# Layer 1's experts: weights in 8 KB pieces with tokens in that order, and tokens of seven of eight pairs fetched by indirect loads

## The chip, the cores and the metric

The kernel runs on one core of one Trainium2 chip, in float32. The metric is the device time of one execution in microseconds (us), lower is better, given as the median of the runs. TensorE (PE) does the matmuls, VectorE (DVE), ScalarE (ACT) and GpSimd (POOL) the elementwise work, and SyncE (SP) issues most of the transfers between HBM and the on-chip memory. 16 DMA engines carry the transfers of all queues.

## The reference

Two layers over 256 latent tokens and 256 context tokens of width 1024. Each layer has a mixer and then a mixture of experts. This case touches the second layer's experts alone, which see the 256 latent tokens: the router gives each token two experts of 16, and an expert is three matrices in a gated unit: gate and up of 1024 by 512, down of 512 by 1024.

```python
    combine = jnp.sum(jax.nn.one_hot(expert_idx, N_EXPERTS, dtype=jnp.float32) * wts[..., None], axis=1)

    def expert(acc, p):
        wg, wu, wd, gate_col = p
        y = (jax.nn.silu(t @ wg) * (t @ wu)) @ wd
        return acc + gate_col[:, None] * y, None
```

The input of the experts is `hl = rmsnorm(xl, norm_ffn_g) * (1 + m[4]) + m[3]`, and after them come a gated residual and a final RMSNorm.

## The kernel before

One core does the whole of both layers in one program, whose instruction order on each engine is written out by hand: generators that `step()` advances between blocks of matmuls, and from L2524 on plain loops.

**The weights' stream.** `Stream` (L28) holds a plan of all weight tiles, in the order of use, and rings of 1 MB buffers. `fill()` issues the next load on SP's queue (L76) as soon as the program has given a buffer back by `done()`; the instruction then waits on the queue until the buffer's last reader is through. `plan_moe(l)` (L218) plans a layer's experts: for layer 1 gate and up in two halves of 512 input rows each (`g`, `u`, halves `kh`), then the down matrix of the expert before, in two halves (`d`). `rows()` (L206) is the layout of a tile: partition p, piece k holds row 128 k + p, so that a partition reads four runs of 512 floats (2 KB) for gate and up and two runs of 1024 floats (4 KB) for down.

**The tokens.** `router_pair` (L1311) multiplies the residual stream by the norm's gain rows into `xg_hu[0]` and `xg_hu[1]` (128 tokens each; POOL, L1324), transposes the stream and makes the router's scores. `moe_row` (L1372) finishes a row tile: ACT scales it by the norm's root (L1376) and POOL adds the shift rows (L1377); the second tile is done by DVE in `row_half` (L2554), as work beside `route` (L1566), which makes ranks and weights.

**The experts.** Experts go in pairs; each has CAP = 64 slots. `which` (L2534) makes a pair's one-hot tile on DVE. `slots1` (L2570) turns it by four small matmuls into a token number and a weight for each slot (`tw`; an empty slot's number is out of range). `gather1` (L2584) multiplies the token tiles by the one-hot tile, 16 matmuls that leave the pair's tokens transposed in two PSUM tiles, which ACT copies to `x` (L2596). `hidden_half` (L2599) multiplies `x` by gate and up, `hidden` (L2606) makes silu(gate) times up (L2609, L2610) and transposes it (L2615), `down1` (L2621) multiplies by the down matrix and weighs the result, and `add1` (L2643) adds it to the four residual tiles in PSUM by a one-hot product.

The loop (L2696) runs expert e's gate and up matmuls, then the down matmuls of expert e-1, then `add1` of e-2. After expert e = 0, 2, ... 12 it runs `slots_of1`, `gather_of` and `ranks_of` for the pairs ahead:

```python
        if e % 2 == 0 and e < NEXP - 2:
            slots_of1(e // 2 + 1)
            gather_of(e // 2 + 1)
            ranks_of(e // 2 + 2)
```

Pair 0 is gathered before the loop (L2691). After it, a block that runs only if an expert has over 64 tokens (L2731, not entered with these inputs), and the final norm. Layer 0's experts fetch their tokens by indirect loads from a copy in HBM: `gather` (L1716) on POOL's queue, 96 slots each.

Of the kernel before, what the change touches and what calls it, by code (L numbers as in the profile page):

```python
# [89 lines left out]
def build(tc, I, out):  # L90
# [115 lines left out]
    def rows(ap, r0, n, c0, w):  # L206
        return ap[r0:r0 + 128 * n, c0:c0 + w].rearrange("(k p) c -> p k c", p=128)

    w_in = I["ab_w_in"][0]
    w_out = I["ab_w_out"][0]  # L210
# [7 lines left out]
    def plan_moe(l):  # L218
        def down(e):
            for hf in range(2):  # L220
                if l:
                    S.add(("d", l, e, hf), rows(I["moe_w_down"][l, e], 256 * hf, 2, 0, D))
                else:
                    S.add(("d", l, e, hf), rows(I["moe_w_down"][l, e], 0, 4, 512 * hf, 512))
        gu = (("g", "moe_w_gate"), ("u", "moe_w_up"))
        for e in range(NEXP):
            for (n, w), kh in [(x, kh) for kh in range(2) for x in gu] if l else [(x, kh) for x in gu for kh in range(2)]:
                S.add((n, l, e, kh), rows(I[w][l, e], 512 * kh, 4, 0, 512))
            if e:
                down(e - 1)  # L230
        down(NEXP - 1)
# [1078 lines left out]

    def router_pair(X, streams, xg, pr, hf):  # L1311

# [7 lines left out]
        if hf and pr == 0:  # L1320
            RT["l"] = yield from (ANY if len(streams) > 2 else YS).take()
            SC.activation(epsc[:, 1:2], epsc[:, 0:1], AF.Sqrt)
        for t in ts:
            GP.tensor_tensor(xg[t][:, sl], X[t][:, sl], RT["g", i][:, sl], op=ALU.mult)  # L1324
        pp = []
# [1156 lines left out]
    hwt2 = lambda name, shape, bufs=1, dt=F32: tw.tile(list(shape), dt, name=name, tag=name, bufs=bufs)  # L2482
    xg_hu = [hu[3][:, D * t:D * t + D] for t in range(2)]
    tail["otl"], tail["oth"] = hwt2("otl", [128, 8, 256], dt=F32R), hwt2("oth", [128, 8, 256], dt=F32R)
    P.release()
    P.ahead()

    def out_add(hf, a):
        sl = slice(512 * hf, 512 * hf + 512)
        tmp = quarter(hu, 9 + a)  # L2490
        DV.tensor_tensor(tmp, accs[hf, a].ap, m2[:, sl], op=ALU.mult)
        accs[hf, a].done()
        DV.tensor_tensor(X[2 + a][:, sl], X[2 + a][:, sl], tmp, op=ALU.add)
        if a:
            g = router_pair(X[2:4], [0, 0], xg_hu, 0, hf)
            if hf:
                begin(g)
            else:
                pend.append(lambda: begin(g))
# [43 lines left out]
    S.ring([rows_g], last=moe_last[1])  # L2543
    moe_row(xg_hu, 0, 0, 0)
    S.ring([unit(wbase, f"wb{i}") for i in range(2)] + [unit(hw, f"hu{i}") for i in range(6, 7)], last=moe_last[1])
# [8 lines left out]
    def row_half(hf):  # L2554
        v, sl = xg_hu[1][:, 512 * hf:512 * hf + 512], slice(512 * hf, 512 * hf + 512)
        DV.scalar_tensor_tensor(v, v, rs[:, 1:2], RT["s", 0][:, sl], op0=ALU.mult, op1=ALU.add)

# [3 lines left out]
    S.ring([rows_s], last=moe_last[1])  # L2561
    h = [xg_hu[t].rearrange("p (k c) -> p k c", k=8) for t in range(2)]
    gh, itok = (hp.tile([128, n], F32, name=m, tag=m, bufs=1) for m, n in (("masksr", 512), ("masks", T)))
# [6 lines left out]
    def slots1(oh, cols):  # L2570
# [11 lines left out]
        yield tw  # L2582

    def gather1(oh, n):  # L2584

        n_x[0] += 1
        x = xy[:, 1024 * (n_x[0] % 2):1024 * (n_x[0] % 2) + 8 * n * CAP].rearrange("p (k i l) -> p k i l", k=8, i=n)
        for kh in range(2):
            p = ps_tr()
            pv = p[:, 0:4 * n * CAP].rearrange("p (k i l) -> p k i l", k=4, i=n)  # L2590
            for k in range(4):
                for t in range(2):
                    mm(pv[:, k], h[t][:, 4 * kh + k], oh[:, t, 0:n, 0].bitcast(F32), k == 0 and t == 0, t == 1)
                if k % 2:
                    yield
            SC.activation(x[:, 4 * kh:4 * kh + 4], pv, AF.Copy)  # L2596
            yield None if kh else x
# [8 lines left out]
    def hidden(acc):  # L2606

        s_, up = mt("sg", [128, 512]), slice(CAP, 2 * CAP)
        SC.activation(s_[up], acc[0:CAP], AF.Silu)  # L2609
        DV.tensor_tensor(s_[up], s_[up], acc[up], op=ALU.mult)  # L2610
        for _ in range(4):
            yield
        p = ps_tr()
        for c in range(4):
            PE.transpose(p[:, CAP * c:CAP * c + CAP], s_[up, 128 * c:128 * c + 128], ident[up, up])  # L2615
        yield
# [79 lines left out]
    for e in range(NEXP + 1):  # L2696
# [21 lines left out]
        if e > 1:  # L2718
            add1(*ZB.pop(e - 2), False)
        if e % 2 == 0 and e < NEXP - 2:  # L2720
            slots_of1(e // 2 + 1)
            gather_of(e // 2 + 1)
            ranks_of(e // 2 + 2)
        if e == 9:
# [6 lines left out]
    with tc.If(most > CAP):  # L2731
# [3 lines left out]
        with tc.For_i(0, NEXP, 1) as e:  # L2735
# [4 lines left out]
            def weights(w, r0, n):  # L2740
                nw[0] += 1
                t = wov[nw[0] % 2].rearrange("p (k c) -> p k c", k=n)
                SY.dma_start(t, I[w][1][bass.ds(e, 1), r0:r0 + 128 * n, :].rearrange("o (k p) c -> p (o k) c", p=128))
                return t

            for b in range(1, T // CAP):
# [4 lines left out]
                tw = tw[:, 0]  # L2751
                x = next(v for v in list(gather1(oh, 1)) if v is not None)[:, :, 0]
                acc = ps_y()
# [63 lines left out]
```

## Time and profile before

| | before |
|---|---|
| median of 3 runs | 1573.33 us (1572.43 to 1574.84) |
| the profiled execution: time, span | 1573.54 us, 1571.7 us |
| PE busy, share of the span | 1402.3 us, 89% |
| DVE, ACT, POOL busy | 931.9, 755.9, 641.1 us |
| HBM read, written | 329.12 MB, 11.37 MB |
| queue of SP and ACT loads: packets, MB | 176112, 323.69 MB |
| queue of POOL's transfers | 4208, 8.90 MB |

An engine's busy time is a mean over stages with different limits. The experts of layer 1 run from about 1333 to 1558 us, and what bounds them is read there. A group of instructions made by the helper `mm` has line L99, so that groups are told apart by their tiles: `y` is gate and up, `tr<-...,hT` is down, `tr<-oneh` is the gather, `acc<-z,back` is `add1`. Each float32 matmul stands as two records.

### The profile page before, as it was taken

Reading aid. Unit: us, or ns where it says so; the run is one execution under the profiler, and the core shown is the slowest. Engines: PE = TensorE matmul, PEld = TensorE weight load, DVE = VectorE, ACT = ScalarE, POOL = GpSimd, SP = SyncE. Lnnn points to the kernel's source line nnn. Section 1 sums busy time; section 2 is a strip of 40 time slices with the busy share of each in tenths; the row PEclk is TensorE's granted clock in tenths of the full one; section 3 lists DMA queues with packets and bytes.
Section 4 is the critical chain, followed back from the end, with each engine's and each line's share of the span. In section 5 each row is a group of like instructions: output and inputs, shape, how many; then the busy total and the mean of one; then the engine's idle time right before and its main releaser. Section 6 shows DMA issues by size and latency. Waiting matters only on the chain. (4 is left out here: it accounts for less than half of the span.)

```text
span 1571.7 us, 19457 instructions
## 1 busy us (share of the span) xinstructions
PE 1402.3 (89%) x7312; PEld 940.1 (60%) x7312; DVE 931.9 (59%) x1254; ACT 755.9 (48%) x1269; POOL 641.1 (41%) x398
## 2 busy tenths in 40 slices
PE   5999989796688988899999994899999888999996
PEld 2677755454476665576666761678787665444442
DVE  2675540899396466789999883544554555222223
ACT  4453435363535534588877882644453553121222
POOL 4343324787855374356668551342243223000000
PEclk8999999898899999899999997899999999999998
DMA  9256443553023154899999995422122568999994
GB/s 330 86 148 155 120 119 134 161 188 107 0 75 140 54 216 158 302 368 373 373 372 335 343 371 220 156 81 81 54 71 66 208 220 320 340 395 393 395 393 172
DMA packets 181687, 337.67 MB, mean 215 GB/s; under 512 B 7513, under 2 KB 44641, under 8 KB 181072
## 3 DMA queue, kind: packets, MB, share of 16 engines
q1 hardware_dynamic: 176112, 323.69, 59.4%
q0 software_dynamic: 4208, 8.90, 1.9%
q10 hardware_dynamic: 1264, 3.73, 0.6%
q8 instruction: 61, 1.00, 0.3%
q14 instruction: 42, 0.34, 0.1%
HBM read 329.12 MB, written 11.37 MB: 217 GB/s over the span
## 5 line engine op out<-in xcount | busy, mean ns | idle before, releaser
L475 POOL TENSOR_TENSOR wb<-wring,wb 128x1024 fp32r<-128x1024 f32 x68 | 170.3, 2507 | 277.3 <-ACT wb L474 234.4
L99 PE MATMUL acc<-hh,wb 128*128 128x512 f32 x640 | 207.3, 400 | 4.0 <-ACT wb L474 2.1
L474 ACT ACTIVATE wb<-wring 128x1024 fp32r<-128x1024 f32 x90 | 94.8, 1058 | 106.0 <-PE acc L99 58.9
L99 PEld LDWEIGHTS acc<-hh,wb 128*128 128x128 f32 x640 | 119.2, 188 | 39.1 <-issue 6.0
L99 PE MATMUL acc<-wb,um 128*96 128x512 f32 (+1 forms) x480 | 122.8, 402 | 5.9 <-DVE wb L475 2.9
L99 PE MATMUL acc<-hl,wb 128*128 128x512 f32 x320 | 126.8, 396 | 0.3 <-DVE hl L600 0.2
L717 DVE SCALAR_TENSOR_TENSOR ca<-u,pcol,ca 128x572 f32<-128x572 f32 x87 | 109.7, 1319 | 0.0
L99 PEld LDWEIGHTS acc<-wb,um 128*96 128x96 f32 (+1 forms) x480 | 79.1, 169 | 38.8 <-DVE wb L475 6.2
L2778 POOL TENSOR_TENSOR xl<-xl,fg 128x512 f32<-128x512 f32 x1 | 1.3, 1264 | 242.4 <-ACT xl L2777 242.4
L99 PE MATMUL y<-hu,hu 128*64 128x512 f32 (+2 forms) x296 | 85.6, 522 | 2.9 <-DVE hu L2161 2.8
L2610 DVE TENSOR_TENSOR sg<-sg,y 64x512 f32<-64x512 f32 x16 | 11.1, 692 | 120.6 <-ACT sg L2609 120.6
L475 POOL TENSOR_TENSOR um<-wring,um 128x1024 fp32r<-128x1024 f32 x17 | 53.8, 3162 | 55.4 <-ACT um L474 53.1
L99 PE MATMUL acc<-um,um 128*96 128x512 f32 (+2 forms) x272 | 69.3, 395 | 2.8 <-POOL um L475 2.8
L99 PEld LDWEIGHTS acc<-hl,wb 128*128 128x128 f32 x320 | 60.1, 188 | 15.2 <-DVE hl L600 1.6
L475 DVE TENSOR_TENSOR wb<-uo,wb 128x1024 fp32r<-128x1024 f32 x32 | 60.6, 1927 | 9.7 <-ACT wb L474 9.3
L99 PE MATMUL acc<-uo,um 128*96 128x512 f32 (+1 forms) x240 | 62.9, 400 | 0.0
L475 POOL TENSOR_TENSOR um<-uo,um 128x1024 fp32r<-128x1024 f32 x18 | 50.3, 2796 | 26.7 <-ACT um L474 26.6
L869 DVE SCALAR_TENSOR_TENSOR xa<-xin,pcol,xa 128x514 f32<-128x514 f32 x64 | 58.7, 918 | 2.3
L2609 ACT ACTIVATE sg<-y 64x512 f32<-64x512 f32 x16 | 9.4, 589 | 96.9 <-PE y L99 96.9
L99 PEld LDWEIGHTS y<-hu,hu 128*64 128x64 f32 (+2 forms) x296 | 32.0, 152 | 38.1 <-issue 33.1
L99 PEld LDWEIGHTS acc<-um,um 128*96 128x96 f32 (+1 forms) x272 | 43.7, 177 | 17.9 <-POOL um L475 5.6
L99 PE MATMUL acc<-wb,hxh 128*128 128x512 f32 x160 | 52.7, 411 | 0.0
(666 smaller groups left out, 3503.6 us busy)
## 6 DMA issues: line engine op xcount, KB each, us to landing
wring<-in_mod_w_dram SPq DMA_DIRECT2D x32, 1024.0 KB, 5.4
uo<-in_moe_w_down_dram SPq DMA_DIRECT2D x19, 1024.0 KB, 14.9
wring<-in_moe_w_gate_dram SPq DMA_DIRECT2D x16, 1024.0 KB, 14.2
hu<-in_moe_w_gate_dram SPq DMA_DIRECT2D x16, 1024.0 KB, 13.7
uo<-in_moe_w_up_dram SPq DMA_DIRECT2D x13, 1024.0 KB, 10.0
wring<-in_moe_w_up_dram SPq DMA_DIRECT2D x13, 1024.0 KB, 9.1
wring<-in_hg_w_in_dram SPq DMA_DIRECT2D x13, 1024.0 KB, 5.1
hu<-in_moe_w_down_dram SPq DMA_DIRECT2D x13, 1024.0 KB, 12.7
```

Of the source, the lines that this page charges most:

```text
L99: PE.matmul(o, l, r, start=start, stop=stop, skip_group_check=True)
L474: SC.activation(hv, w, AF.Copy)
L475: eng.tensor_tensor(lv, w, hv.bitcast(F32), op=ALU.subtract)
L717: DV.scalar_tensor_tensor(a, x, w, a, op0=ALU.mult, op1=ALU.add)
L869: DV.scalar_tensor_tensor(a[:, 0:514], x[:, k:k + 514], par("sc_w", 16 * k + i), a[:, 0:514], op0=ALU.mult, op1=ALU.add)
L2609: SC.activation(s_[up], acc[0:CAP], AF.Silu)
L2610: DV.tensor_tensor(s_[up], s_[up], acc[up], op=ALU.mult)
L2778: GP.tensor_tensor(o, o, fg[hf], op=ALU.mult)
```

## The change

For layer 1 only:

- `rows_p` gives the weight tiles another layout: partition p holds n neighbouring rows (n = 4 for gate and up, 2 for down), so that it reads one run of 8 KB. Partition p, piece k of gate and up is now row 512 kh + 4 p + k, so the tokens' columns are put in that order: `by4` views are given to `router_pair`, to the pass over `xg_hu[0]` (written out in place of `moe_row`) and to `row_half`. These read their inputs with a step of four floats and write contiguously. In `hidden` the views `sv`, `av` put the 512 hidden values in the down matrix's order.
- The two token tiles are stored to a new HBM tile `hD1` by POOL's queue, after `route`.
- For pairs 1 to 7, `fetch` takes the place of `gather_of`: two small DVE copies of the slot numbers and one indirect load of 128 rows of 4 KB into `xg1` (the buffer of the first token tile). After the next (odd) expert, `turn` transposes it, eight transposes into two PSUM tiles, copied to `x` by ACT as before. Pair 0 keeps the gather.
- In the block for experts with over 64 tokens the same is done.

The core of the diff:

```diff
+    def rows_p(ap, r0, n):
+        return ap[r0:r0 + 128 * n, :].rearrange("(p k) c -> p k c", k=n)
...
-                    S.add(("d", l, e, hf), rows(I["moe_w_down"][l, e], 256 * hf, 2, 0, D))
+                    S.add(("d", l, e, hf), rows_p(I["moe_w_down"][l, e], 256 * hf, 2))
...
-                S.add((n, l, e, kh), rows(I[w][l, e], 512 * kh, 4, 0, 512))
+                S.add((n, l, e, kh), rows_p(I[w][l, e], 512 * kh, 4) if l else rows(I[w][l, e], 512 * kh, 4, 0, 512))
...
+        order = perm or (lambda x: x)
         for t in ts:
-            GP.tensor_tensor(xg[t][:, sl], X[t][:, sl], RT["g", i][:, sl], op=ALU.mult)
+            o = xg[t][:, sl]
+            GP.tensor_tensor(perm(o, True) if perm else o, order(X[t][:, sl]), order(RT["g", i][:, sl]), op=ALU.mult)
...
+    def by4(x, put=False):
+        return x.rearrange("p (k q) -> p k q", k=4) if put else x.rearrange("p (q k) -> p k q", k=4)
...
-    moe_row(xg_hu, 0, 0, 0)
+    SC.activation(xg_hu[0], xg_hu[0], AF.Copy, scale=rs[:, 0:1])
+    for hf in range(2):
+        v = by4(xg_hu[0][:, 512 * hf:512 * hf + 512], True)
+        GP.tensor_tensor(v, v, by4(RT["s", 0][:, 512 * hf:512 * hf + 512]), op=ALU.add)
...
-        v, sl = xg_hu[1][:, 512 * hf:512 * hf + 512], slice(512 * hf, 512 * hf + 512)
-        DV.scalar_tensor_tensor(v, v, rs[:, 1:2], RT["s", 0][:, sl], op0=ALU.mult, op1=ALU.add)
+        v, sl = by4(xg_hu[1][:, 512 * hf:512 * hf + 512], True), slice(512 * hf, 512 * hf + 512)
+        DV.scalar_tensor_tensor(v, v, rs[:, 1:2], by4(RT["s", 0][:, sl]), op0=ALU.mult, op1=ALU.add)
...
+    hD1 = dram.tile([T, D], F32, name="hD1")
+    xg1 = xg_hu[0]
+    for t in range(2):
+        GP.dma_start(hD1[128 * t:128 * t + 128, :], xg_hu[t])
...
+    def fetched(tw):
+        ig, n = mt("ig", [128, 1], 2, I32), CAP * len(tw)
+        for i, v in enumerate(tw):
+            DV.tensor_copy(ig[CAP * i:CAP * i + CAP], v[CAP * i:CAP * i + CAP, 0:1])
+        GP.indirect_dma_start(out=xg1[0:n], out_offset=None, in_=hD1[:, :],
+                              in_offset=bass.IndirectOffsetOnAxis(ap=ig[0:n, :1], axis=0),
+                              bounds_check=T - 1, oob_is_err=False)
...
+    def turned(n):
+        n_x[0] += 1
+        r = n * CAP
+        x = xy[:, 1024 * (n_x[0] % 2):1024 * (n_x[0] % 2) + 8 * r].rearrange("p (k i l) -> p k i l", k=8, i=n)
+        for kh in range(2):
+            p = ps_tr()
+            for k in range(4):
+                PE.transpose(p[:, r * k:r * k + r], xg1[0:r, 512 * kh + 128 * k:512 * kh + 128 * k + 128], ident[0:r, 0:r])
+            SC.activation(x[:, 4 * kh:4 * kh + 4], p[:, 0:4 * r].rearrange("p (k i l) -> p k i l", k=4, i=n), AF.Copy)
+        return x
...
-        SC.activation(s_[up], acc[0:CAP], AF.Silu)
-        DV.tensor_tensor(s_[up], s_[up], acc[up], op=ALU.mult)
+        sv, av = s_.rearrange("p (h k q) -> p h k q", h=2, k=2), acc.rearrange("p (h q k) -> p h k q", h=2, k=2)
+        SC.activation(sv[up], av[0:CAP], AF.Silu)
+        DV.tensor_tensor(sv[up], sv[up], av[up], op=ALU.mult)
...
-        if e % 2 == 0 and e < NEXP - 2:
-            slots_of1(e // 2 + 1)
-            gather_of(e // 2 + 1)
-            ranks_of(e // 2 + 2)
+        if e < NEXP - 2:
+            if e % 2:
+                turn(e // 2 + 1)
+            else:
+                slots_of1(e // 2 + 1)
+                fetch(e // 2 + 1)
+                ranks_of(e // 2 + 2)
```

## Rows read from the trace of the kernel before

**Rows 1.** Windows: us, engine busy us, PE clock, DMA share, GB/s.

```profile
1333.00:1350.00 17.00, 15.56 (x92) 7.91 (x90) 1.68 (x5) 4.10 (x7) 0.00 (x0) 1.00 0.73 272
1350.00:1545.00 195.00, 195.00 (x1018) 87.51 (x1016) 48.91 (x92) 39.47 (x70) 0.00 (x0) 1.00 1.03 391
```

**Rows 2.** Chain of waits, layer 1's experts: start us, us, what.

```profile
1441.44 7.02 PE y L99 x32
1448.46 3.43 PE tr L99 x16
...
1453.41 4.23 PE tr L99 x36
...
1469.61 0.87 PE tr L2676 x8
...
1538.78 7.02 PE y L99 x32
```

**Rows 3.** Timeline of SP's queue: start us, us, what.

```profile
1523.40 2.63 SPq L76 DMA_DIRECT2D wb<-in_moe_w_up_dram  x1
```

**Rows 4.** DMA issues, 1524 to 1526 us: KB, us to landing.

```profile
wb<-in_moe_w_up_dram SPq DMA_DIRECT2D x1, 1024.0 KB, 14.5
```

**Rows 5.** Windows with DMA idle time.

```profile
1335.57:1338.48 2.91, 2.91 (x18) 0.91 (x14) 0.00 (x0) 0.00 (x0) 0.00 (x0) 1.00 0.22 38
...
1350.00:1351.50 1.50, 1.50 (x10) 0.52 (x8) 0.00 (x0) 0.00 (x0) 0.00 (x0) 1.00 0.38 44
...
1544.80:1547.40 2.60, 2.60 (x16) 0.89 (x14) 0.69 (x1) 0.59 (x1) 0.00 (x0) 1.00 0.62 251
```

**Rows 6.** DMA rate of 1350 to 1545 us, 40 slices.

```profile
GB/s 245 386 408 387 387 405 392 386 397 401 387 393 402 388 387 408 390 385 401 397 387 395 400 387 391 405 389 388 402 393 386 398 397 388 389 409 386 386 408 406
```

**Rows 7.** Timeline, boundary after expert 12: start us, us, what.

```profile
1509.41 1.20 PE L99 MATMUL acc<-z,back 128*128 128x512 f32 x4
...
1510.45 0.50 PE L99 MATMUL tr<-rv,oneh 128*128 128x4 f32 x4
...
1510.81 4.03 PE L99 MATMUL tr<-oneh,hu 128*128 128x128 f32 x32
1511.12 0.63 ACT L2639 ACTIVATE z<-yo 64x512 fp32r<-64x512 f32 x1
...
1512.45 0.15 DVE L2580 TENSOR_SCALAR tw<-tr 128x2 f32<-128x2 f32 x1
...
1512.88 0.60 ACT L2596 ACTIVATE hu<-tr 128x512 f32<-128x512 f32 x1 [1.14 <-PE tr L99]
```

**Rows 8.** DMA queues, 692.74 to 735.33 us: packets, MB, share.

```profile
q1 hardware_dynamic: 7398, 14.69, 95.4%
q0 software_dynamic: 448, 1.15, 8.4%
```

**Rows 9.** Source line L1717, layer 0's fetches: ns min/median/max.

```profile
L1717 POOL DMA_INDIRECT um<-hD,ig x16: 986/1776/1850, 632.3 to 890.9; - x16
...
DMA to landing us min/median/max: 4.4/8.3/9.8
```

**Rows 10.** Timeline ahead of the experts, POOL and DVE.

```profile
1313.04 1.29 POOL L1324 TENSOR_TENSOR hu<-xl,rows_g 128x512 f32<-128x512 f32 x1 [2.58 <-DVE xl L2493]
...
1313.67 1.22 DVE L2493 TENSOR_TENSOR xl<-xl,hu 128x512 f32<-128x512 f32 x1
...
1320.25 2.34 POOL L1377 TENSOR_TENSOR hu<-hu,rows_s 128x1024 f32<-128x1024 f32 x1 [3.28 <-ACT hu L1376]
1320.30 2.84 DVE L2556 SCALAR_TENSOR_TENSOR hu<-hu,rs,rows_s 128x512 f32<-128x512 f32 x1
```

**Rows 11.** Source lines L2377 and L2618, ACT: ns min/median/max.

```profile
L2377 ACT ACTIVATE oth<-tr x4: 630/644/670, 1289.1 to 1292.4; 128x256 fp32r<-128x256 f32 x4
...
L2618 ACT ACTIVATE hT<-tr x16: 383/385/386, 1341.8 to 1549.7; 128x256 f32<-128x256 f32 x16
```

**Rows 12.** Page, part 5, DVE in hidden(): busy us, mean ns.

```profile
L2610 DVE TENSOR_TENSOR sg<-sg,y 64x512 f32<-64x512 f32 x16 | 11.1, 692 | 120.6 <-ACT sg L2609 120.6
```

More of the change, by code (lines that the diff above doesn't have):

```diff
@@ L1309, in router_pre, with router_pair @@
         RT["rows"] = True
-    def router_pair(X, streams, xg, pr, hf):
+    def router_pair(X, streams, xg, pr, hf, perm=None):
         ts, i = (2 * pr, 2 * pr + 1), streams[2 * pr]
@@ L2494, in out_add @@
         if a:
-            g = router_pair(X[2:4], [0, 0], xg_hu, 0, hf)
+            g = router_pair(X[2:4], [0, 0], xg_hu, 0, hf, by4)
             if hf:
@@ L2561, in build @@
     S.ring([rows_s], last=moe_last[1])
-    h = [xg_hu[t].rearrange("p (k c) -> p k c", k=8) for t in range(2)]
+    h = [xg_hu[t].rearrange("p (h k q) -> p h k q", h=2, k=4) for t in range(2)]
+    hD1 = dram.tile([T, D], F32, name="hD1")
+    xg1 = xg_hu[0]
+    for t in range(2):
+        GP.dma_start(hD1[128 * t:128 * t + 128, :], xg_hu[t])
     gh, itok = (hp.tile([128, n], F32, name=m, tag=m, bufs=1) for m, n in (("masksr", 512), ("masks", T)))
@@ L2582, in slots1, with fetch, turn @@
         yield tw
+    def fetch(q):
+        fetched([TW[2 * q + i] for i in range(2)])
+    def fetched(tw):
[5 more added lines that the diff above has]
+                              bounds_check=T - 1, oob_is_err=False)
+    def turn(q):
+        x = turned(2)
+        XT1.update({2 * q + i: x[:, :, i] for i in range(2)})
+    def turned(n):
[8 more added lines that the diff above has]
+        return x
     def gather1(oh, n):
@@ L2592, in gather1 @@
                 for t in range(2):
-                    mm(pv[:, k], h[t][:, 4 * kh + k], oh[:, t, 0:n, 0].bitcast(F32), k == 0 and t == 0, t == 1)
+                    mm(pv[:, k], h[t][:, kh, k], oh[:, t, 0:n, 0].bitcast(F32), k == 0 and t == 0, t == 1)
                 if k % 2:
@@ L2614, in hidden @@
         for c in range(4):
-            PE.transpose(p[:, CAP * c:CAP * c + CAP], s_[up, 128 * c:128 * c + 128], ident[up, up])
+            PE.transpose(p[:, CAP * c:CAP * c + CAP], sv[up, c // 2, c % 2], ident[up, up])
         yield
@@ L2742, in weights @@
                 t = wov[nw[0] % 2].rearrange("p (k c) -> p k c", k=n)
-                SY.dma_start(t, I[w][1][bass.ds(e, 1), r0:r0 + 128 * n, :].rearrange("o (k p) c -> p (o k) c", p=128))
+                SY.dma_start(t, I[w][1][bass.ds(e, 1), r0:r0 + 128 * n, :].rearrange("o (p k) c -> p (o k) c", k=n))
                 return t
@@ L2751, in build @@
                 tw = tw[:, 0]
-                x = next(v for v in list(gather1(oh, 1)) if v is not None)[:, :, 0]
+                fetched([tw])
+                x = turned(1)[:, :, 0]
                 acc = ps_y()
```

## The prediction

> **What bounds the kernel now.** The change lies in the last stage, the experts of layer 1, so that stage is what I read: first its windows, then the chain through it, then its last loads, then the DMA's rates. The windows view [rows 1] says two things of 1350 to 1545 us: PE is busy for all 195.00 of 195.00 us, and the 16 DMA engines are full too (share 1.03, 391 GB/s). Two full resources mean that neither share tells the bound; the order of events does. The chain of waits [rows 2] goes through PE alone: one pair of experts takes 28.17 us (1441.44 to 1469.61), and each of its two experts starts its 7.02 us of gate and up matmuls with no wait. A pair needs 12 loads of 1 MB. At the rates below these take 31.96 us, more than PE's 28.17, so the stage lives on the lead it has when it starts: 19 loads are issued before expert 0. The lead shrinks by 3.8 us a pair. How much is left? The last "up" load is issued at 1523.40 [rows 3] and lands 14.5 us later [rows 4], at 1537.9; its matmuls are the second half of the piece of the chain that starts at 1538.78, so they start at 1542.3 [rows 2]. 4.4 us of lead remain. The DMA has moved its last byte at some 1546.4 (1544.8 plus 2.6 x 0.62/1.02) [rows 5]. So PE sets the end, the DMA is 4.4 us behind it, and a gain on PE alone is worth 4.4 us at most. The change works on both.
>
> **Pieces of 8 KB.** The rate line of this stretch, 40 slices of 4.9 us [rows 6], swings between 385 to 388 and 405 to 409 GB/s; loads come as four of gate and up (runs of 2 KB) and two of down (runs of 4 KB). So 1 MB takes 1.0486/0.387 = 2.71 us in 2 KB pieces and 1.0486/0.408 = 2.57 us in 4 KB pieces. Per engine (32 and 16 pieces) that is 84.7 and 160.6 ns a piece, that is 75.9 ns for 2 KB and 8.8 ns for each piece whatever its size. An 8 KB piece then takes 4 x 75.9 + 8.8 = 312.4 ns, and 1 MB 2.50 us. No row has weights in such pieces, so the bounds are 2.50 (the line through both rows) and 2.57 (nothing beyond 4 KB); I take 2.50, since both rows lie on a fixed cost for each piece. Of the 77 loads that follow the first 19, 49 save 0.21 and 28 save 0.07 us: 12.3 us; of the 73 up to the last up load, 12.0 us. On this point the Trainium skill speaks against the change: "DMA: Bandwidth & Descriptors", section Specifications, gives 512 B as the smallest transfer that runs at line rate, by which 2 KB and 8 KB would be the same. The trace disagrees: 387 against 408 GB/s for pieces that are both far above that size.
>
> **The gather leaves PE.** At every second expert boundary PE makes the slot numbers and then the gather: 4.23 us [rows 2], of which the slots' four matmuls take 0.4 and the gather's 16 (32 records) the rest [rows 7]. The slots stay. In place of the gather, eight transposes stand at the other boundary; eight of that size take 0.87 us [rows 2]. Their results go through two ACT copies of 0.60 us, and ACT is not free: its last z copy ends at 1511.12 + 0.63 = 1511.75, while PE is done with the boundary's last acc matmul at 1510.6 [rows 7]. PE waits for the first copy alone: 1511.75 + 0.60 + 0.05 = 1512.4, so the boundary grows by 1.8 us. A pair saves 4.23 - 0.4 - 1.8 = 2.0 us, seven pairs 14.0. Bounds: transposes alone (0.9, seven save 20.3), both copies (2.4, seven save 9.8). What hides the second copy is expert e+1's first half; without it, it would cost 0.6.
>
> **What is added to the DMA.** Seven fetches of 128 slots; only slots that hold a token are in bounds, 512 token rows over 8 pairs, so 64 rows of 4 KB each. By bytes that is 0.64 us at 408 GB/s. Layer 0 shows the price: from 692.74 to 735.33 (42.59 us, always full) the hardware queue moved 14.69 MB and the software queue 1.15 MB [rows 8]; two fetches and two scatters run in it. 14.69 MB at 387 GB/s take 38.0 us, so these four, of 70 rows each, cost 4.6 us, or 1.06 for 64 rows. Bounds: 0.64, and 1.3 (the 64 rows on 8 of the 16 engines: 8 pieces of 160.6 ns); I take 1.1, since layer 0's is the same kind of transfer: 7.7 us. The store of 1 MB to hD1 (some 2.6 us) is issued by POOL at some 1326.5, behind the second row_half; the ring is then full, and the DMA idles from 1335.57 to 1338.48 (share 0.22) [rows 5], which covers it; uncovered it costs 2.6. Behind these two issues POOL has only the iota L2564, first used by expert 0's results. No other queue is moved past: SP issues the same loads in the same order. On the other side the DMA stalls now, as in 1350.00 to 1351.50 (share 0.38) [rows 5], since expert 1's buffers come free only after a gather of 3.8 us. That gather is gone, so I count 2.5 us of early DMA idle time as regained (1.0 to 3.2).
>
> **Is a fetch back in time?** The transposes stand in PE's queue; behind them is the next expert. Its index is written by DVE at 1512.45 [rows 7], two copies of some 0.15 follow, so POOL starts at 1512.9. The transposes are due one expert later (7.02 + 3.43 + 1.5 us [rows 2]), at 1522.8: 9.9 us. In layer 0 a fetch lands 8.3 us after its issue in the median and 9.8 at most [rows 9]. It fits, with little to spare.
>
> **Ahead of the stage.** Reading with a step of 16 bytes may make L1324 on POOL longer. Two of its four (1.30 us) hold DVE's L2493 back, which takes 1.22 instead of 0.69 and lies on the chain [rows 10]. No POOL row has such a step; the nearest are two ACT copies of 256 elements, 0.64 us with a step and 0.385 without [rows 11], 1.65 times. So 1.30 becomes 1.30 to 2.15; I take +0.4 each, 0.8 in all. The skill's "GPSIMD Engine Reference", section 7, says +50% for reads with a step over 8 bytes; by it the two would cost 1.3. No run here shows it yet. Then row_half(0) (L2556, 2.84 us) waits for POOL's L1377 (2.34 us) [rows 10], now two instructions: if DVE gets in between them it gains up to 1.1 us, if it waits for both at the longer time it loses up to 1.9; I take +0.4. Together +1.2 (-1.1 to +3.6). This shifts PE and DMA alike, since the DMA waits for PE's first release. In hidden() the strided ACT and DVE pass (0.69 us [rows 12]) grow by under 1 us together, hidden by 3.43 us of down matmuls [rows 2]; only expert 0 has none.
>
> **The sum.** PE alone: -14.0 + 1.2 = -12.8, so it wants the last up load at 1542.3 - 12.8 = 1529.5. That load lands at 1537.9 - 12.0 + 7.7 - 2.5 + 1.2 = 1532.3. PE waits 2.8 us in all, mostly over the last experts, and the end moves by -12.8 + 2.8 = -10.0. The profiled execution took 1573.54 (span 1571.7 and 1.8 around it), the median of the runs is 1573.33; 1573.5 - 10 gives 1563.6. After the change the DMA, not PE, is late. With all bounds good (transposes 0.9, fetch 0.64, idle 3.2, -1.1) PE wants that load at 1520.9 and has it at 1526.1: -21.4 + 5.2 = -16.2, or 1557. With all bad (2.4, 1.3, 1.0, +3.6) it wants it at 1536.1 and has it at 1537.6: -6.2 + 1.5 = -4.7, or 1569.
>
> **Rivals.** First, pieces of 8 KB run like those of 4 KB, because they are cut or nothing is left to save: 49 x 0.14 = 6.9 instead of 12.0 us, the wait grows to 7.9, the end is -4.9, 1568.6. For it: no row has such weights. Against: a fixed cost for each piece fits both rows. Second, no piece gains at all, which is also the case that the change doesn't do what it says: the load lands at 1544.3, PE waits 14.8, the end is +2.0, 1575.5; this is the skill's rule above. The two rates speak against it. Third, slower: a fetch comes too late for its transposes. Place: PE's queue at seven boundaries. Each us beyond 9.9 costs 7 us, less the 2.8 that PE waits anyway; from a landing time of 11.7 us it eats PE's whole gain, and at 12.5 the end is +5.4, 1579. For it: 128 slots' descriptors instead of 96, and 8 KB pieces to wait behind at every turn. Against: layer 0's 9.8 at most, beside a DMA as full.
>
> **How the numbers follow.** Forecast 0.60 (1557 to 1569 by itself), 4 KB rival 0.17, no gain 0.06, late fetch 0.10, and 0.07 for a longer start or a PE whose clock falls in the new waits (1.00 in the whole stage now [rows 1]). A measurement of this kernel tells 0.2%, some 3 us, from no change. Faster: 0.60 + 0.17 + 0.05 = 0.82; same 0.08; slower 0.10. The range takes in the first rival and some of the rest: 1557 to 1571.5.
>
> **What would show it.** Landings of weight loads 2.50 us apart (419 GB/s), packets of 8 KB; the 32 gather records gone from all seven boundaries; PE waiting for weights in the last four experts, 2 to 3 us in all; fetches that land 8 to 10 us after issue with no PE wait on them; L1324 at 1.3 to 2.1 us; the first expert 1.2 us later. Wrong would be: 2.57 us a load, POOL instructions of over 2.6 us, or PE waiting for xg1.

## The result, and the profile after

The changed kernel takes 1564.46 us (median of 8 runs, 1562.38 to 1570.11) against 1573.15 us before: ratio 0.9947, 95% interval 0.9931 to 0.9963. That is 8.7 us less, where 10.0 less were forecast; so the forecast of 1563.6 us came within 1 us, and the range holds. Its profiled execution took 1567.05 us (span 1565.2). The steps behind the number hold less well than the number, so the profile is read at the places that the forecast named.

The stage is easiest to compare from a point ahead of every engine instruction that the change edits: the end of the last VectorE pass of line 479 (475 in the kernel before). From there to the end of the span it took 265.9 us before and 260.5 us after, and second profiles of both kernels (last experiments below) give 266.0 and 260.4. So the stage itself gives 5.5 us and not 10.0. What is left of the 8.7 lies ahead of that pass, whose end falls anywhere between 1298 and 1308 us in the profiles of this study; 5.5 us is a ratio of 0.9965, inside the interval of the second timing of the changed kernel (0.9942 to 0.9969) and just outside that of the first. Whether the rest belongs to the change can be asked of the first four experiments below, which were timed in one batch: their medians differ from before by +7.1, -0.8, -8.2 and -8.4 us, their stages by +7.1, +0.1, -8.7 and -8.4. There the stage is the whole difference, to 0.9 us. In the two timings of the change the medians give some 3 us more than the stage.

The page of the changed kernel first: the DMA rate in 40 slices of the span, and the packets by size.

```profile
GB/s 332 86 153 153 121 117 135 162 189 107 2 66 150 54 215 155 292 372 374 373 373 333 346 372 210 164 82 79 80 56 81 170 261 273 366 420 420 420 421 172
...
DMA packets 154311, 340.56 MB, mean 218 GB/s; under 512 B 8105, under 2 KB 45233, under 8 KB 141408
```

Four whole slices of the stage stand at 420 GB/s, where [rows 6] swung between 385 and 409. Now the windows (us, engine busy us, PE clock, DMA share, GB/s): the first pair's gather, expert 1's gate and up, and the stage from its third expert on.

```profile
1331.00:1333.00 2.00, 2.00 (x12) 2.00 (x10) 0.00 (x0) 0.19 (x1) 0.00 (x0) 0.50 1.03 430
...
1347.10:1350.40 3.30, 3.30 (x11) 0.84 (x8) 0.47 (x2) 0.00 (x0) 1.11 (x1) 0.50 1.02 429
...
1361.00:1545.00 184.00, 178.25 (x874) 71.78 (x876) 50.97 (x105) 39.37 (x72) 5.96 (x6) 1.00 0.98 408
```

Against [rows 1] PE is no longer full (178.25 of 184 us), DMA nearly is (0.98), and twice at the start PE runs at a granted clock of 0.50, its 1.2 GHz level, where it had 1.00 at the same work before ([rows 1] for expert 1; for the first pair's gather this window of the kernel before):

```profile
1327.20:1331.00 3.80, 3.75 (x34) 3.78 (x34) 1.15 (x8) 0.60 (x1) 0.00 (x0) 1.00 1.05 393
```

The chain of waits through one pair (start us, us, what):

```profile
1399.65 7.02 PE y L99 x32
1406.67 3.43 PE tr L99 x16
...
1411.47 0.64 ACT z L2685
...
1412.12 0.63 ACT z L2688
...
1412.78 0.61 ACT hu L2628
...
1413.42 7.09 PE y L99 x32
1420.51 3.43 PE tr L99 x16
...
1425.80 4.43 PE y L99 x19
```

A pair takes 1425.80 - 1399.65 = 26.15 us where [rows 2] has 28.17. The 4.23 us of gather are gone from the chain; in their place it leaves PE for ScalarE's two z copies and the first copy of the turn, as forecast. What PE waits for from expert 0 to the end of the stage (us in total, times, longest):

```profile
PE y L99 <- ACT hu L2628: 5.5, 6, 0.9
PE tr L2664 <- DVE sg L2659: 1.4, 1, 1.4
PE tr L2725 <- ACT hu L2628: 0.9, 1, 0.9
PE tr L2627 <- ACT hT L2667: 0.5, 1, 0.5
```

No line names a DMA. The last "up" load is issued at 1511.16 and takes 20.6 us (SP's queue, and the DMA view of that stretch):

```profile
1511.16 0.33 SPq L76 DMA_DIRECT2D wb<-in_moe_w_up_dram  x1
```

```profile
wb<-in_moe_w_up_dram SPq DMA_DIRECT2D x1, 1024.0 KB, 20.6
```

It lands at 1531.8. Its matmuls are the second half of the chain's piece `1531.14 7.02 PE y L99 x32`; on the timeline they start at 1534.56, so the load is 2.8 us early (2.9 in the expectations below), where the forecast had PE waiting 2.8 us for it. Last, the stretch ahead of the experts, where [rows 10] stood, POOL and then VectorE (the timeline):

```profile
1312.75 2.12 POOL L1330 TENSOR_TENSOR hu<-xl,rows_g 128x512 f32<-128x512 f32 x1 [1.75 <-DVE xl L2504]
...
1321.22 3.84 POOL L2558 TENSOR_TENSOR hu<-hu,rows_s 128x512 f32<-128x512 f32 x2 [2.88 <-ACT hu L2555]
```

```profile
1313.38 2.04 DVE L2504 TENSOR_TENSOR xl<-xl,hu 128x512 f32<-128x512 f32 x1
...
1321.28 2.39 DVE L2570 SCALAR_TENSOR_TENSOR hu<-hu,rs,rows_s 128x512 f32<-128x512 f32 x1
1323.60 1.51 DVE L1588 TENSOR_TENSOR sel<-sco,rbias 128x32 f32<-128x32 f32 x1
...
1327.33 1.12 DVE L2570 SCALAR_TENSOR_TENSOR hu<-hu,rs,rows_s 128x512 f32<-128x512 f32 x1
```

L1330 (L1324 before) takes 2.12 us instead of 1.30 and holds VectorE's L2504 for 2.04 instead of 1.22. A VectorE pass of 32 elements, L1588 (L1582 before), takes 1.51 us, beside the second half of POOL's L2558; before it took 0.18.

### The profile page after: what moved, and what is told of

The parts are those of the page before. It is cut to its first block, busy times and chain, and to the rows that moved or that the text cites. A ratio compares the mean times of both kernels' runs of the same rounds, so it can differ in the third digit from the quotient of the medians.

```text
span 1565.2 us, 19174 instructions
## 1 busy us (share of the span) xinstructions
PE 1383.8 (88%) x7144; PEld 920.0 (59%) x7144; DVE 937.0 (60%) x1268; ACT 755.2 (48%) x1269; POOL 653.7 (42%) x408
## 5 line engine op out<-in xcount | busy, mean ns | idle before, releaser
L479 POOL TENSOR_TENSOR wb<-wring,wb 128x1024 fp32r<-128x1024 f32 x68 | 170.1, 2504 | 275.4 <-ACT wb L478 232.5
L99 PE MATMUL acc<-hh,wb 128*128 128x512 f32 x640 | 207.3, 401 | 4.0 <-ACT wb L478 2.1
L99 PEld LDWEIGHTS acc<-hh,wb 128*128 128x128 f32 x640 | 119.2, 188 | 39.1 <-issue 6.0
L99 PE MATMUL acc<-wb,um 128*96 128x512 f32 (+1 forms) x480 | 122.8, 402 | 5.9 <-DVE wb L479 2.9
L99 PE MATMUL acc<-hl,wb 128*128 128x512 f32 x320 | 126.9, 396 | 0.3 <-DVE hl L604 0.2
L99 PEld LDWEIGHTS acc<-wb,um 128*96 128x96 f32 (+1 forms) x480 | 79.2, 169 | 38.7 <-DVE wb L479 6.0
L99 PE MATMUL y<-hu,hu 128*64 128x512 f32 (+2 forms) x296 | 85.0, 519 | 4.6 <-DVE hu L2167 2.7
L2611 POOL DMA_INDIRECT hu<-hD,ig x7 | 7.1, 1010 | 172.4 <-DVE ig L2610 154.4
L2659 DVE TENSOR_TENSOR sg<-sg,y 64x512 f32<-64x512 f32 x16 | 11.1, 692 | 106.8 <-ACT sg L2658 106.8
L99 PE MATMUL acc<-um,um 128*96 128x512 f32 (+2 forms) x272 | 69.1, 394 | 2.8 <-POOL um L479 2.8
L99 PEld LDWEIGHTS acc<-hl,wb 128*128 128x128 f32 x320 | 60.1, 188 | 15.2 <-DVE hl L604 1.6
L99 PE MATMUL acc<-uo,um 128*96 128x512 f32 (+1 forms) x240 | 62.9, 400 | 0.0
L99 PEld LDWEIGHTS y<-hu,hu 128*64 128x64 f32 (+2 forms) x296 | 31.5, 150 | 39.5 <-issue 33.6
L99 PEld LDWEIGHTS acc<-um,um 128*96 128x96 f32 (+1 forms) x272 | 43.6, 176 | 17.8 <-POOL um L479 5.7
L99 PE MATMUL acc<-wb,hxh 128*128 128x512 f32 x160 | 52.7, 411 | 0.0
## 6 DMA issues: line engine op xcount, KB each, us to landing
hu<-in_moe_w_down_dram SPq DMA_DIRECT2D x13, 1024.0 KB, 10.5
```

The lines of the kernel that those rows point to most:

```text
L99: PE.matmul(o, l, r, start=start, stop=stop, skip_group_check=True)
L479: eng.tensor_tensor(lv, w, hv.bitcast(F32), op=ALU.subtract)
L2611: GP.indirect_dma_start(out=xg1[0:n], out_offset=None, in_=hD1[:, :], in_offset=bass.IndirectOffsetOnAxis(ap=ig[0:n, :1], axis=0), bounds_ ...
L2659: DV.tensor_tensor(sv[up], sv[up], av[up], op=ALU.mult)
```

## Experiments

All are compared in one table. Times are medians in us, with the ratio to the kernel before timed beside each; the other columns are read from the profiles, in us after the end of that last pass of line 479 (475): where expert 0's and expert 15's first gate matmul starts, where the last up load lands (for one kernel the trace has no landing, and the start of the matmul that waits for it stands instead), and the end of the span. 3.5 us after expert 15's start PE wants that load.

| kernel | time (ratio, 95%) | expert 0 | expert 15 | last up load | end |
|---|---|---|---|---|---|
| before | 1573.15 | 27.0 | 232.9 | 232.1 | 265.9 |
| before, again | one run | 27.0 | 232.9 | 232.3 | 266.0 |
| the change | 1564.46 (0.9931-0.9963) | 32.0 | 226.4 | 227.1 | 260.5 |
| the change, again | 1565.26 (0.9942-0.9969) | 32.1 | 226.5 | 227.2 | 260.4 |
| pieces alone | 1578.76 (1.0028-1.0061) | 32.1 | 239.6 | 225.9 | 273.0 |
| fetch alone | 1570.79 (0.9979-1.0008) | 28.0 | 227.0 | 235.3 | 266.0 |
| natural order, PE strided | 1563.44 (0.9930-0.9967) | 30.9 | 223.6 | 225.9 | 257.2 |
| turn ahead | 1563.22 (0.9934-0.9969) | 32.2 | 220.1 | 227.2 | 257.5 |
| natural order, old pieces for two experts | 1559.27 (0.9891-0.9928) | 27.0 | 219.7 | 221.8 | 253.6 |
| the same, turn ahead | 1557.91 (0.9886-0.9928) | 28.7 | 217.1 | 223.9 | 254.1 |
| every fetch twice | one run | 32.1 | 226.5 | 232.5 | 263.7 |
| the change, PE kept busy | 1560.43 (0.9912-0.9958) | 30.1 | 222.8 | 225.0 | 256.9 |
| natural order, turn ahead, PE kept busy | 1558.84 (0.9887-0.9936) | 27.0 | 216.4 | by 223.1 | 253.3 |

**Pieces alone.** The 8 KB pieces and the permuted order stay; every pair is gathered on TensorE.

```diff
-                turn(e // 2 + 1)
...
-                fetch(e // 2 + 1)
+            gather_of(e // 2 + 1)
```

> Half of the change alone: 8 KB pieces and the permuted tokens stay, but every pair is gathered on TensorE again; no store of the tokens, no fetch, no turn. Theory A (PE sets the end of the stage, the loads are close behind it): the loads run at 420 GB/s and lie idle early, PE keeps its 28.17 us a pair, and the passes ahead of the first expert, 3.4 to 5 us longer, are all that is left: 1576 to 1578.5 us against 1573.2. Rival B (the loads set the end of before): the 12 us that 73 loads save show, less the later start: 1564 to 1567. Signs: the stretch from one pair's gather to the next (28.2 by A, near 26.2 by B), and whether the last up load lands more than 10 us ahead of the first matmul that reads it (A) or just before it (B).

Slower than before, as theory A has it (1578.76 us is 0.3 above its range): the chain has the old pair again,

```profile
1375.18 7.02 PE y L99 x32
...
1387.15 7.02 PE y L99 x32
...
1399.11 4.22 PE tr L99 x36
1403.34 1.86 PE y L99 x7
```

28.16 us, and the loads' gain is spent waiting: the last up load lands 17.2 us before PE wants it (239.6 + 3.5 - 225.9). What remains is the start, 5.1 us later, and 1.6 us between experts 0 and 1, where the half clock now falls into the second pair's gather.

**Fetch alone.** Weights in their old pieces, tokens in natural order.

```diff
-        S.add(("d", l, e, hf), rows_p(I["moe_w_down"][l, e], 256 * hf, 2))
+        S.add(("d", l, e, hf), rows(I["moe_w_down"][l, e], 256 * hf, 2, 0, D))
...
-    g = router_pair(X[2:4], [0, 0], xg_hu, 0, hf, by4)
+    g = router_pair(X[2:4], [0, 0], xg_hu, 0, hf)
```

> The other half alone: tokens fetched by indirect loads and turned, weights in their old 2 KB and 4 KB pieces, tokens in natural order, so that none of the passes ahead of the first expert is longer. Theory A (both bounds lie close together, so taking the gather off PE gains nothing while the loads go at the old rate): the last up load lands at the old 1537.9 us less 2.5 of early idle plus 6 fetches of 0.93, 1541, where PE would want it at 1528.3: 1571.5 to 1574.5 us, the same as before, with PE waiting for loads in the later experts. Rival B (PE alone sets the end): PE's 14 us a whole are gained, 1559 to 1561.

No difference that is measured, as theory A has it; in the clock of the kernel before, the last up load lands at 235.3 + 1305.8 = 1541.1, and 1541 was expected. That it fits so well is in part luck: expert 0 starts 1.0 us later than before, because the first gather ran at the half clock here too (its line stands in the part on the clock), and that was not in the expectation. PE's waits show the bound change hands:

```profile
PE y L99 <- DMA wb<-in_moe_w_up_dram: 1.7, 1, 1.7
PE y L99 <- DMA rows_g<-in_moe_w_up_dram: 1.7, 1, 1.7
PE y L99 <- DMA hrl<-in_moe_w_up_dram: 1.6, 1, 1.6
...
PE y L99 <- DMA hu<-in_moe_w_up_dram: 1.1, 1, 1.1
```

These two runs settle the frame of the forecast: two bounds lie close together, either half of the change moves one of them and gains nothing, and both halves gain. They also price the pieces: with the old ones the load lands 8.1 us later although expert 0 starts 4.0 us earlier, so 12.1 us; the sum had 12.0.

**Natural order, strided reads on TensorE.** No permuted writes on POOL and VectorE; TensorE takes every fourth column as its weights.

```diff
-    h = [xg_hu[t].rearrange("p (h k q) -> p h k q", h=2, k=4) for t in range(2)]
+    h = [xg_hu[t].rearrange("p (h q k) -> p h k q", h=2, k=4) for t in range(2)]
```

> The whole change, but the tokens stay in natural order in SBUF and TensorE reads every fourth column as its weights (in the gather of the first pair and in the turns) in place of the writes in permuted order by POOL and VectorE. Theory A (the later start is the price of the permuted passes on POOL and VectorE): expert 0 starts 3.4 to 5 us earlier, all pairs keep 26.15 us: 1559 to 1561 us against 1564.5 for the whole change, and PE begins to wait for the last loads by up to 1.5 us. Rival B (the start is late for another reason, the clock among them): 1563.5 to 1565. Rival C (a strided read of weights costs TensorE what it cost POOL): the gather of the first pair and each turn grow by over 1 us, 1565 or more.

Between A and C. Routing is back at its old time, but the first pair's gather now costs what that gave (PE by operation and shape; first this kernel, then the one further below that has old pieces for experts 0 and 1 and reads rows):

```profile
L99 PE MATMUL tr<-oneh,hu 128*128 128x128 f32 x32 | 7.7, 399 | 1.4 <-DVE q L1620 1.4
```

```profile
L99 PE MATMUL tr<-oneh,hu 128*128 128x128 f32 x32 | 3.8, 278 | 1.4 <-DVE q L1620 1.4
```

3.9 us more for the gather, so expert 0 starts only 1.1 us earlier than with the change. The turns read the same way at no cost: a pair still takes 26.15 us. And the 0.50 clock in the gather and in expert 1 is absent in this profile: expert 0's start to expert 15's takes 192.7 us and not 194.4, half of the 3.3 us (260.5 - 257.2).

**Turn ahead.** Slots, fetch and turn move ahead of ScalarE's and VectorE's work at each expert's end.

```diff
             if g:
                 HT1[e] = last_of(g)
+            if e < NEXP - 2:
+                if e % 2:
+                    turn(e // 2 + 1)
+                else:
+                    slots_of1(e // 2 + 1, ps_y)
+                    fetch(e // 2 + 1)
```

> The whole change, with the slots, the fetch and the turn put ahead of the work on ScalarE and VectorE at the end of each expert, so that the turn's PSUM copy no longer stands behind the copies of the weighted outputs. Theory A (what is left at the boundary is PE waiting 0.9 us for that copy, and the loads land 2.9 us ahead of PE): seven turns give 6 us to PE, of which the loads let through about 3: 1560.5 to 1562.5 us against 1564.5, and PE waits for the last loads by some 3 us. Rival B (the wait only moves to the outputs' copies, which now stand behind the turn): 1564 to 1566. Rival C (the loads do not set the end at all): the full 6, 1558 to 1559.

In the stage theory A holds: 3.0 us less than the change, and PE's waits for the turn's copy give way to waits for loads.

```profile
PE y L99 <- DMA wb<-in_moe_w_up_dram: 2.0, 1, 2.0
...
PE y L99 <- DMA rows_g<-in_moe_w_up_dram: 0.4, 1, 0.4
PE y L99 <- ACT hu L2628: 0.3, 1, 0.3
```

The time (1563.22) lies between the ranges of A and B and does not separate them: its interval is nearly that of the change. So after the change the loads are not late, but under 3 us from it.

**The change, again** (no edit).

> The changed kernel once more, unedited, as the companion of the next three and as a second profile of its start. From the end of the last VectorE pass of line 479 to the end of the span its first profile has 260.5 us and that of the kernel before 265.9. Theory A (the later start and TensorE's half clock after it belong to the change): 260 to 261.5 again, expert 0 starting 32.0 us after that pass, and granted clock 0.50 while expert 1's gate and up run. Rival B (the half clock was an accident of that execution): 257 to 259, with expert 1's gate and up at 7.09 us and not 8.78.

Theory A: the end, the start and expert 1's half clock repeat to 0.1 us.

**Natural order, with old pieces for experts 0 and 1.** Only the first pair's gather needs the tokens in the weights' order; so its eight gate and up loads go back to 2 KB pieces and the tokens stay in rows.

```diff
-                S.add((n, l, e, kh), rows_p(I[w][l, e], 512 * kh, 4) if l else rows(I[w][l, e], 512 * kh, 4, 0, 512))
+                S.add((n, l, e, kh), rows_p(I[w][l, e], 512 * kh, 4) if l and e > 1 else rows(I[w][l, e], 512 * kh, 4, 0, 512))
...
-    PE.transpose(p[:, r * k:r * k + r], xg1[0:r, 512 * kh + 128 * k:512 * kh + 128 * k + 128], ident[0:r, 0:r])
+    PE.transpose(p[:, r * k:r * k + r], by4(xg1[0:r, 512 * kh:512 * kh + 512])[:, k], ident[0:r, 0:r])
```

> The whole change, but tokens in natural order in SBUF, and the gate and up weights of experts 0 and 1 alone in their old 2 KB pieces, so that the first pair's gather reads its tokens in rows (no permuted pass on POOL or VectorE, no strided weight read on TensorE); the turns of the other pairs read every fourth column on TensorE. Theory A (the start is what the change lost): expert 0 starts 27 to 28 us after the last pass of line 479, as before, against 32.0; the first loads after it are released 4 us earlier, so the last up load lands at 223.5 to 224.5 us after that pass, where PE wants it at 224.3; that pass to the end of the span 254 to 255.5 us, a time 5 to 6.5 us under the whole change's: 1557.5 to 1560. Rival B (the loads' end is fixed by something else than expert 0's start): the last up load lands at 226 as with the tokens in natural order and every weight in 8 KB pieces, PE waits for it, 256.5 or more.

Theory A, and a little more than it asked: 253.6 us, 6.9 less than the change; 1559.27 us against 1565.26 for the change timed beside it. Ahead of the experts the rows of before are back (POOL, then VectorE),

```profile
1313.32 1.30 POOL L1330 TENSOR_TENSOR hu<-xl,rows_g 128x512 f32<-128x512 f32 x1 [2.57 <-DVE xl L2504]
```

```profile
1313.95 1.22 DVE L2504 TENSOR_TENSOR xl<-xl,hu 128x512 f32<-128x512 f32 x1
...
1323.34 0.18 DVE L1588 TENSOR_TENSOR sel<-sco,rbias 128x32 f32<-128x32 f32 x1
```

and expert 1's gate and up run at full clock (window):

```profile
1342.50:1349.70 7.20, 7.20 (x35) 2.51 (x37) 1.28 (x6) 0.01 (x1) 1.11 (x1) 1.00 1.01 415
```

The loads follow expert 0's earlier start, and are 1.3 us ahead of PE at the last up load (they land at 221.85, and its matmuls start at 223.17).

**The same with the turn ahead.** Both edits together.

> The kernel with the natural order and the old pieces for experts 0 and 1, and the slots, fetch and turn ahead of ScalarE's and VectorE's work at each expert's end as well. Theory A (both bounds by now lie within 1 us of each other, so the second edit can give only what the loads leave): that pass of line 479 to the end 253.5 to 255 us, under 1 us less than with the first edit alone, PE waiting for the last up load by 4 to 5 us. Rival B (PE sets the end): 249 to 251, all of the seven turns' waits.

The stage ends 0.5 us later than without the second edit, PE waiting 3.4 us in expert 15 (its 32 matmuls take 10.5 us, not 7.1). Rival B is out. Theory A's size can't be read off it, since here PE had its 0.50 clock in the first gather and in expert 1, natural order or not.

**Every fetch twice.** The second goes into space that nothing reads.

```diff
+        if twice:
+            GP.indirect_dma_start(out=xg_hu[1][0:n], out_offset=None, in_=hD1[:, :],
+                                  in_offset=bass.IndirectOffsetOnAxis(ap=ig[0:n, :1], axis=0), ...)
```

> The whole change with each pair's fetch issued twice, the second into tokens' space that nothing reads any more: a price for one fetch in the stream of loads. Theory A (a fetch takes the room of its bytes in the stream, 0.93 us by the landings of the whole change): the last up load lands 6 times 0.9 = 5.6 us later, 232.7 us after the last pass of line 479 in place of 227.1, and PE waits for it by some 2.7 us. Rival B (a fetch runs beside the loads in time that they leave): the last up load lands within 1 us of 227.1.

Theory A: the last up load lands 5.4 us later, and a wait appears. The expectation counted six fetches ahead of that load; all seven are issued before it, so one costs 0.77 us:

```profile
PE y L99 <- DMA wb<-in_moe_w_up_dram: 1.3, 1, 1.3
```

The stage ends 3.2 us later: the 5.4 less the lead of 2.8 that the change had, so 2.6 (expert 15's matmuls take 9.7 us, not 7.1; the list of waits shows only half of it), and 0.6 at the very end (below).

**The change, with TensorE kept busy.** 18 transposes of the identity, into a tile that nobody reads, where PE stood idle: 8 between the routing's counts and the first gather, 10 between expert 0's gate and up and its transposes.

```diff
+    def fill(n):
+        p = ps_y()
+        for _ in range(n):
+            PE.transpose(p[:, 0:128], ident, ident)
```

> The whole change with 18 transposes of the identity, which nobody reads, where TensorE stands idle before the half-clock stretches: 8 between the routing's counts and the first pair's gather, 10 between expert 0's gate and up and its transposes. Theory A (those pauses of TensorE, 1.8 and 1.3 us, bring the granted clock down): expert 1's gate and up take 7.09 us in place of 8.78, the last pass of line 479 to the end of the span is 257.5 to 259 in place of 260.4, and the time 1.5 to 3 us under the whole change's. Rival B (the clock comes down for what lies further back): 8.78 us again and 260 to 261.5.

Theory A, by more than it asked: the first gather and expert 1 have the full clock (windows of the stretch ahead of the experts with the gather, and of expert 1's gate and up),

```profile
1320.00:1330.00 10.00, 7.24 (x55) 5.79 (x54) 6.75 (x37) 1.19 (x2) 2.28 (x4) 1.00 1.00 397
...
1340.20:1347.30 7.10, 7.10 (x35) 2.49 (x36) 1.29 (x6) 0.00 (x0) 1.11 (x1) 1.00 1.01 391
```

and the stage is 3.5 us shorter with work added: expert 0 starts 1.95 us earlier, expert 1 takes 1.7 us less. But that the transposes kept the clock up is not shown. From 18.9 to 21.9 us after that pass the granted clock is 0.50 in the change and 1.00 here (windows, the change first), and the first added transpose runs after that stretch:

```profile
1323.60:1326.60 3.00, 3.00 (x5) 1.20 (x4) 2.93 (x18) 0.00 (x0) 2.10 (x2) 0.50 1.00 423
```

```profile
1319.60:1322.60 3.00, 2.06 (x5) 0.67 (x4) 2.93 (x19) 0.00 (x0) 1.75 (x2) 1.00 1.01 426
```

```profile
1323.22 1.07 PE L2575 MATMUL y<-ident 128*128 128x128 f32 x8
```

So this execution had taken another course before the added work began, it is one profile, and the times do not tell either (0.9912 to 0.9958, beside 0.9942 to 0.9969 for the change). What stays is a price: with the full clock in the gather the start is 30.1 - 27.0 = 3.1 us late, which is left for the permuted passes.

**Natural order, turn ahead, TensorE kept busy.** The two edits and the 18 transposes.

> The kernel with natural order, old pieces for experts 0 and 1 and the early turn, with the same 18 transposes. Theory A: no half clock in the first pair's gather or in expert 1, expert 0 starts 27 us after that pass of line 479 and not 28.7, the last up load lands at 222 and not 223.9, 252 to 253 us to the end in place of 254.1. Rival B: half clock as before, 254 to 255.

No half clock in the gather or in expert 1 and expert 0 at 27.0, as theory A has it; but natural order with old pieces has the same without the transposes. The last up load is some 1 us later than the 222 of theory A, the end, 253.3, is 0.3 over its range, and only 0.3 below the natural order with old pieces by itself, because now loads are waited for at four places (0.5 to 1.3 us each in the list of waits). The three natural kernels with old pieces for two experts end within 0.8 us of each other: the two with the turn ahead wait for loads, the third is 1.3 us from it, and their times (1557.9 to 1559.3) can't be told apart. Natural order with old pieces for experts 0 and 1 is the simplest of the three.

**Before, again** (no edit).

> The kernel before once more, unedited, for a second profile of its last stage: all readings of what a kernel gains from the last VectorE pass of line 475 (479 in the changed kernel) to the end of the span rest on one profile of it, 265.9 us. Theory A (the stage takes the same time in every execution, and what differs between executions lies ahead of that pass): 265.4 to 266.4, expert 0 starting 27.0 us after that pass. Rival B (the stage itself varies as the whole does, by some 3 us): 263 to 269.

Theory A: 266.0. As far as two profiles tell, the variation between executions lies ahead of that pass.

## Why the prediction was right, and where it was not

*Two close bounds: right.* The two halves alone show it better than any row of before could: 1.0044 and 0.9993, together 0.9947.

*Pieces of 8 KB: right.* 2.50 us a load was taken; loads land 2.47 to 2.50 us apart at 420 GB/s, and the pieces are worth 12.1 us by the landings. The rivals of 4 KB speed and of no gain fall with it, and so does the rule of the Trainium skill ("DMA: Bandwidth & Descriptors", section Specifications) that would give 2 KB pieces the line rate already: 387 GB/s against 420.

*The gather off PE: right.* 2.0 us a pair were taken, 28.17 - 26.15 = 2.02 measured. Over the stage, expert 0's start to expert 15's shrinks from 205.9 to 192.7 us where no half clock falls in it, 13.2 of the 14.0; the first pair, whose turn has a longer wait, gives less.

*Fetches: right.* 0.77 us each by doubling them (1.1 taken, so the seven were put 2.3 us too high; 0.64 by bytes), landing 8.3 us after issue and 8.5 at most (8.8 in the change's second profile), inside the 9.9:

```profile
DMA to landing us min/median/max: 6.0/8.3/8.5
```

PE never waits for xg1, so the slower rival does not occur. The store of hD1 lands by 1337.6 us, ahead of the first release at 1340.4: hidden, as taken.

*The start: the term that was mis-sized.* +1.2 us was taken (at most +3.6), +5.0 came. Step by step from the timeline, against before: the scores are ready 2.1 us later, because L1330 came out at the upper bound (2.12 for 1.30, 1.64 times; +0.4 each had been taken) and L2504 behind it lost 0.82 twice, and because the router's first block of matmuls met the 0.50 clock (1.08 us for 0.64); L1588 ends another 0.9 later; the second L2570 adds 0.4; and the first pair's gather, at 0.50 clock, 1.6. Without the clock that is 2.9, inside the bounds. That L1330 came out so near the upper bound of 1.65 is luck: the two rows behind it [rows 11] are ScalarE copies, and the step in L2377 is one of 64 floats in what it writes, not of four in what it reads. For row_half the forecast saw that L2570 might get in between POOL's two instructions. It did, and won 0.45 us (2.39 for 2.84), but the second POOL instruction then held L1588, the next in VectorE's queue, for 1.3: the forecast followed one VectorE instruction and not its successor. The Trainium skill's +50% ("GPSIMD Engine Reference", section 7) lies below the measured 1.64 times.

*The clock: left out of the sum.* A fall was named with a chance of 0.07 and no price. By rows at either level it costs 3.7 us: 0.4 in the router, 1.6 in the first gather (5.44 us for 3.81), both part of the start above, and 1.7 in expert 1 (8.78 for 7.09). What brings it down stays open. All five profiles with the permuted passes and no added transposes have it in the first gather and again from 42 to 46 us after that pass; but natural order has it too, in the gather with fetch alone, and in both places with old pieces and the turn ahead, while before (twice) and the two other natural-order kernels without added transposes have it in neither. The two natural-order kernels with it are those in which PE ran the router at 1.00 and then stood idle for 2.4 us ahead of the routing's counts, where the others ran it partly at 0.50 and had no such pause; that is an observation on two profiles and not a cause shown. The gather's line in the change and in fetch alone:

```profile
L99 PE MATMUL tr<-oneh,hu 128*128 128x128 f32 x32 | 5.4, 350 | 1.8 <-DVE q L1620 1.8
```

```profile
L99 PE MATMUL tr<-oneh,hu 128*128 128x128 f32 x32 | 5.4, 350 | 1.4 <-DVE q L1620 1.4
```

*The end of the stage: left out.* From expert 15's start to the end is 1.1 us longer (0.8 in the second profiles). 0.74 of it is POOL's last DRAIN before the program closes; the source line of it, before, after, and with every fetch twice:

```profile
L2813 POOLq DRAIN  x3: 46/109/5567, 1565.2 to 1571.4; - x3
```

```profile
L2866 POOLq DRAIN  x3: 46/109/6307, 1558.0 to 1564.9; - x3
```

```profile
L2870 POOLq DRAIN  x3: 46/109/6877, 1561.5 to 1569.0; - x3
```

5.57, 6.31 and 6.88 us; in the whole program POOL issues 51, 60 and 67 transfers there (the change adds seven fetches and the two stores, the last seven fetches more), which is 0.08 us for each, fetch or store. With pieces alone, without either, it is 5.57 again. The rest, 0.1 to 0.4, is hardly more than the 0.2 by which two profiles of one kernel differ there.

*"DMA, not PE, is late": wrong in the changed kernel.* The landing came near: 1532.3 in the clock of before is 226.5 after that pass, and it came at 227.1. That is partly luck, since the start cost 3.8 us more than was taken, the fetches 2.3 less, and by what is left the early idle time gave some 3.4 us back and not 2.5. PE's own time was not 12.8 us earlier but 6.5 (expert 15 at 226.4 for 232.9). The late start is not what kept PE behind the loads, for it moves both, as the prediction says: with natural order on PE, with old pieces for two experts and with PE kept busy expert 0 starts 1.1, 5.0 and 1.95 us earlier, and the last up load lands 1.2, 5.3 and 2.1 us earlier. What moves one against the other is expert 1's half clock (1.7 on PE alone), the pairs (0.8 less than taken), the cheaper fetches (2.3) and the idle time (0.9): together 5.7 us, from the wait of 2.8 that was forecast to the lead of 2.8 that came. Where expert 1 has the full clock the lead is 1.2 to 1.3 us (those three kernels) and not 2.8, and with the turn ahead PE waits.

*The sum.* Forecast: -14.0 + 1.2 + 2.8 = -10.0. Measured in the stage: -13.2 (pairs) + 5.0 (start) + 1.7 (expert 1's clock) + 1.1 (end) + 0 (loads) = -5.4. The time came within 1 us of the forecast because the runs as a whole differ by 8.7, 3.2 more than the stage does in two profiles of each kernel; these 3.2 are not shown to be the change's, so the closeness of the number is luck, while the frame of two close bounds and the prices of pieces and gather are not. The wait that the forecast had at the end did not come; time was lost at the start instead, and that could be removed: natural order with old pieces for two experts ends at -12.3.

## What to carry to other kernels

When two resources run out together, price each half of a change against the other's lead, and look whether one half alone can gain anything: here neither did. A layout that one engine wants is paid by whoever writes it: look which few readers truly need it (here eight loads of 96), and undo it for those. When an instruction on a shared path grows, follow not only the one it blocks but the next in that queue, and read TensorE's granted clock in the stretches behind it.

## What the runs showed of the hardware

- A POOL TENSOR_TENSOR that reads two tiles with a step of 16 bytes took 2.12 to 2.16 us for 512 elements, 1.30 in rows; one such read on VectorE (the second L2570) took 1.12 for 0.74. A VectorE instruction issued beside such a POOL pass was done only after it: L2504 took 2.04 (0.69 with POOL idle), L1588 with its 32 elements 1.51 (0.18).
- TensorE as reader of that step: the gather's 32 records took 7.7 us and not 3.8, while the eight transposes of a turn cost a pair nothing (26.15 us either way). PSUM read by VectorE with a step of 8 bytes cost nothing either, L2659 at the 692 ns of [rows 12].
- The same 32 records of the first gather took 3.81 us at a granted clock of 1.00 and 5.44 us where it was 0.50 for part of them, in kernels with and without the permuted passes. Natural-order kernels, with the same 1.4 us pause of PE ahead of the gather, had either clock, so that pause does not tell it by itself.
- Each transfer that POOL issued, indirect load or store, came with 0.08 us more of POOL's closing DRAIN (5.57, 6.31 and 6.88 us with 51, 60 and 67 of them in the program).
